# Summed K pairs in Up, one ring of split weight tiles and three rows of 512 in a SwiGLU encoder block

## The chip, the cores and the metric

The kernel runs on one core of a Trainium2 chip. The metric is device time in microseconds (us) of one execution; the number given is the median of several runs. Engines: PE is TensorE (matmuls and transposes), DVE the vector engine, ACT the scalar engine, POOL GpSimd, SP the engine whose queue issues the weight transfers here.

## What is computed

One encoder block on 256 tokens of width 2048, in f32: a hybrid attention layer, a cross-attention layer, and then the part that the change touches, the SwiGLU layer with a hidden width of 5632, and a last norm:

```python
def rms_norm(x, g, eps=NORM_EPS):
    xf = x.astype(jnp.float32)
    y = xf * lax.rsqrt(jnp.mean(xf * xf, axis=-1, keepdims=True) + eps)
    return (y * g.astype(jnp.float32)).astype(x.dtype)
...
x = x + (jax.nn.silu(h @ w_gate) * (h @ w_up)) @ w_down     # h = rms_norm(x, g_f)
```

## The kernel before

Every product of two f32 matrices is made of three matmuls on rounded parts (`mm`, L93 to L95): each operand is split into a high part, a cast made by ACT (L101), and a low part, the difference made by DVE (L102); high by high, high by low and low by high are summed in PSUM. Weights come in pieces of 1 MB into three raw buffers `wraw`, by SP's queue in program order. Each piece of 128x2048 is split in two steps of 1024 columns into tiles `wh` and `wl`, which rotate over four buffers each.

SwiGLU cuts the 5632 hidden columns into one narrow chunk of 512 and five wide chunks of 1024. The chunks run in three groups: the narrow and the first wide one, the second and third, the fourth and fifth. A wide chunk is Gate, then Up (`wide_chunk`, L830); a group ends with its share of the down product (`wide_add`, twice).

`narrow_chunk` (L815) runs the narrow Gate project into two PSUM banks (`acc_4196` and `acc_4197` below), then `normalized_pairs` (L784), which scales x by the rows' norm and makes the operand forms that the wide chunks use, then the narrow Up project (`acc_4401`, `acc_4402`). For each half of the tokens it then applies Silu to Gate's bank (`sg`, ACT, L824), multiplies by Up's (`h`, DVE, L826) and transposes (PE, L325).

A wide Gate or Up (`wide_result`, L742, by `wide_project`, L691) works through 8 pairs of K blocks. A string gives the kind of each pair. A plain pair, "P", has two blocks by two of weights: two splits of 128x1024 and 24 matmuls of 512 columns. A summed pair, "W", uses sums of the blocks (a Winograd form with seven products in place of eight): 21 matmuls; three additions on DVE (L719, 1024 columns; L723 and L724, 512 each) make `tsum` from the raw tile, and four pieces are split: `b11` (raw, 1024), `t13` (sums, 1024), `b21` (raw, 512), `t24` (sums, 1024). Four extra PSUM banks Q take the products shared by several results, from the first W pair to the last; then ACT and DVE read them (`leave`), and after the last pair DVE adds the four plain banks (`join`). The split of `t24` goes to a special pair of tiles, `wh2` and `wl2`, of pool `wsum`, since the four rotating ones are taken.

```python
G_KINDS, U_KINDS = "PPWPWPWP", "PPWPWPPP"
...
t24 = split_blocks(t[:, 2:4, :], wsum)
...
return sb.tile([P, 512], F32, name=name, tag="nat", bufs=7)
```

The last line is `nat` (L168): rows of 128x512 for small results, seven of them in rotation. In SwiGLU its users are `rb` and `rrow` (the norm's factors), `sums` (L682 to L685, one for each summed pair of the operand: three in `normalized_pairs`), `sg` and `h`, and in the wide chunks `sums`, `a21`, `v` and `u`. A new row is written only when the readers of the row that had its buffer are done.

The order of instructions on each engine is set by a scheduler when the program is built, from the order of the code and from the buffers; an engine runs its own list in order, and waits by semaphores where another engine must be done.

## Time and profile before

| | before |
|---|---|
| median of 3 runs | 1153.56 us (1152.98 to 1153.72) |
| the profiled execution's own time | 1152.77 us |
| its span in the profile | 1150.9 us |
| mean granted clock | 0.998 |
| PE, matmuls | busy 1141.8 us, 99%, 5495 instructions |
| DVE | busy 910.8 us, 79% |
| ACT | busy 620.5 us, 54% |
| POOL | busy 68.6 us, 6% |
| moved by DMA | 222.13 MB, mean 193 GB/s |

All durations in the trace are of the one profiled execution. Busy time is the time in which an engine has an instruction in work; the duration printed for a matmul is longer than the step to the next, because matmuls overlap in the engine. A row of a timeline gives start and duration; in brackets stands how long the engine had been idle before it, and what ended that.

### The profile page before, as it was taken

To read this page: it belongs to the slowest core of one execution; us is meant where nothing else is said; L and a number is where in the kernel's file an instruction comes from. 1 tells how busy PE (TensorE), PEld (TensorE's weight loads), DVE (VectorE), ACT (ScalarE), POOL (GpSimd) and SP (SyncE) were. 2 spreads that over 40 slices of the span, in tenths; PEclk is the share of its full clock that TensorE was granted. 3 is DMA by queue.
4 is the path that set the end of the run, shared out by engine and by line. 5 is a ranking of instruction groups with operands and counts; after the bars stand their busy time and mean duration, and the time that the engine had idled before them with its cause. 6 is when DMAs were issued, how large, how long until landed. Compare 5 with 4: busy or idle time off the path is not lost.

```text
span 1150.9 us, 14384 instructions
## 1 busy us (share of the span) xinstructions
PE 1141.8 (99%) x5495; PEld 958.6 (83%) x5495; DVE 910.8 (79%) x1206; ACT 620.5 (54%) x875; POOL 68.6 (6%) x81
## 2 busy tenths in 40 slices
PE   9999999999999999999999999999999999999997
PEld 7888888888888888888888888888888888888887
DVE  6688766586868776988888897997888888988873
ACT  7755454554665555665444564664644554654552
POOL 4920000001000000000000000000000000000021
PEclk9999999999999999999999999999999999999999
DMA  9665334445764445455556555555555555565651
GB/s 355 224 209 188 121 137 165 175 147 194 281 220 165 164 147 183 173 195 209 197 183 214 183 204 198 183 197 205 189 214 191 211 188 190 206 226 204 213 201 73
DMA packets 33764, 222.13 MB, mean 193 GB/s; under 512 B 4128, under 2 KB 4896, under 8 KB 8992
## 3 DMA queue, kind: packets, MB, share of 16 engines
q1 hardware_dynamic: 32256, 216.86, 53.3%
q0 software_dynamic: 864, 3.15, 0.8%
q10 hardware_dynamic: 576, 1.21, 0.3%
q8 instruction: 43, 0.70, 0.2%
q14 instruction: 25, 0.20, 0.0%
HBM read 219.11 MB, written 2.10 MB: 192 GB/s over the span
## 4 chain that ended last, share of the span: by engine, by line
PE 98%; issue 0%; DMA 0%; DVE 0%; ACT 0%; POOLq 0%; POOL 0%; DVEq 0%; ACTq 0%
PE acc L93 27%; PE acc L94 27%; PE acc L95 27%; PE q L93 3%; PE q L94 3%; PE q L95 3%; PE pt L325 2%; PE ppt L472 1%; PE psc L95 1%; PE psc L94 1%; PE psc L93 1%; PE acckv L93 0%; PE acckv L94 0%; PE acckv L95 0%; PE pt L848 0%
## 5 line engine op out<-in xcount | busy, mean ns | idle before, releaser
L101 ACT CAST wh<-wraw 128x1024 fp32r<-128x1024 f32 (+2 forms) x399 | 397.4, 1007 | 388.8 <-PE acc L95 343.3
L102 DVE TENSOR_TENSOR wl<-wraw,wh 128x1024 fp32r<-128x1024 f32 (+2 forms) x399 | 466.8, 1180 | 161.3 <-ACT wh L101 159.7
L94 PE MATMUL acc<-wl,x2n_h 128*128 128x512 f32 x320 | 124.8, 391 | 0.0
L95 PE MATMUL acc<-wh,x2n_l 128*128 128x512 f32 x320 | 124.3, 389 | 0.0
L94 PE MATMUL acc<-wl,hT_h 128*128 128x512 f32 (+1 forms) x272 | 103.7, 382 | 0.0
L95 PE MATMUL acc<-wh,hT_l 128*128 128x512 f32 (+1 forms) x272 | 103.2, 380 | 0.0
L93 PE MATMUL acc<-wh,x2n_h 128*128 128x512 f32 x320 | 102.0, 390 | 0.0
L93 PE MATMUL acc<-wh,hT_h 128*128 128x512 f32 (+1 forms) x272 | 88.5, 380 | 0.0
L94 PE MATMUL acc<-wl,x0T_h 128*128 128x512 f32 x224 | 88.0, 394 | 0.0
L93 PE MATMUL acc<-wh,x0T_h 128*128 128x512 f32 x224 | 87.5, 396 | 0.4 <-ACT x0T_h L104 0.4
L95 PE MATMUL acc<-wh,x0T_l 128*128 128x512 f32 x224 | 87.8, 393 | 0.0
L102 DVE TENSOR_TENSOR wl<-tsum,wh 128x1024 fp32r<-128x1024 f32 x66 | 78.8, 1221 | 8.7 <-ACT wh L101 8.7
L101 ACT CAST wh<-tsum 128x1024 fp32r<-128x1024 f32 x66 | 67.2, 1047 | 17.8 <-PE acc L95 8.1
L93 PEld LDWEIGHTS acc<-wh,x2n_h 128*128 128x128 f32 x320 | 60.1, 188 | 12.5
L95 PEld LDWEIGHTS acc<-wh,x2n_l 128*128 128x128 f32 x320 | 60.1, 188 | 12.3
L94 PEld LDWEIGHTS acc<-wl,x2n_h 128*128 128x128 f32 x320 | 60.1, 188 | 12.2
L93 PEld LDWEIGHTS acc<-wh,hT_h 128*128 128x128 f32 x272 | 51.2, 188 | 9.7
L94 PEld LDWEIGHTS acc<-wl,hT_h 128*128 128x128 f32 x272 | 51.2, 188 | 9.5
L95 PEld LDWEIGHTS acc<-wh,hT_l 128*128 128x128 f32 x272 | 51.2, 188 | 9.4
L94 PE MATMUL acc<-wl,forms_h 128*128 128x512 f32 (+1 forms) x155 | 59.0, 384 | 0.0
L95 PE MATMUL acc<-wh,forms_l 128*128 128x512 f32 (+1 forms) x155 | 58.7, 384 | 0.0
L93 PE MATMUL acc<-wh,forms_h 128*128 128x512 f32 (+1 forms) x155 | 56.1, 384 | 0.0
(369 smaller groups left out, 2218.9 us busy)
## 6 DMA issues: line engine op xcount, KB each, us to landing
wraw<-in_w_gate SPq DMA_DIRECT2D x44, 1024.0 KB, 4.8
wraw<-in_w_up SPq DMA_DIRECT2D x44, 1024.0 KB, 4.8
wraw<-in_w_dn SPq DMA_DIRECT2D x36, 1024.0 KB, 4.9
wraw<-in_w_in SPq DMA_DIRECT2D x24, 1024.0 KB, 4.8
wraw<-in_w_out SPq DMA_DIRECT2D x16, 1024.0 KB, 4.8
wraw<-in_w_down SPq DMA_DIRECT2D x8, 1024.0 KB, 4.8
wraw<-in_w_in_lat SPq DMA_DIRECT2D x7, 832.0 KB, 8.3
wraw<-in_w_xk SPq DMA_DIRECT2D x4, 1024.0 KB, 6.3
```

What stands on the lines that cost most here:

```text
L93: nc.tensor.matmul(o, l.h, r.h, start=start, stop=False)
L94: nc.tensor.matmul(o, l.h, r.l, start=False, stop=False)
L95: nc.tensor.matmul(o, l.l, r.h, start=False, stop=stop)
L101: last_cast[0] = nc.scalar.copy(out=dst.h, in_=src).ins
L102: last_split[0] = nc.vector.tensor_tensor(out=dst.l, in0=src, in1=dst.h.bitcast(F32), op=ALU.subtract).ins
L325: nc.tensor.transpose(out=pt[:, j * P:(j + 1) * P], in_=src[:, j * P:(j + 1) * P], identity=ident)
L472: nc.tensor.transpose(out=pt[:, kt * S + tt * P:kt * S + (tt + 1) * P], in_=p[:, tt, kt * P:(kt + 1) * P], identity=ident)
```

## The change

Up gets the same kinds as Gate: three summed pairs instead of two. Gate takes its pairs in their natural order, Up as 0 2 1 4 3 6 5 7, which by kinds is P W P W P W P P, so that two plain ones come last. The high and the low tiles of split weights come from one ring each, in strict rotation: four tiles up to the end of the attention layers, and six in SwiGLU, where two more are taken from a new pool `late`; the special tiles go, and `t24` takes tiles of the ring as the others do. The rows of `nat` come from pool `early`, seven, until the attention layers are closed, and then from `late`, three. Up's weights are laid out on the host by the new kinds.

```diff
--- before.py
+++ after.py
@@ -36,7 +36,9 @@
 NFC = FF // 512
 NPC = (FF - 512) // 1024
 
-G_KINDS, U_KINDS = "PPWPWPWP", "PPWPWPPP"
+GU_KINDS = "PPWPWPWP"
+G_ORDER, U_ORDER = (0, 1, 2, 3, 4, 5, 6, 7), (0, 2, 1, 4, 3, 6, 5, 7)
 
 DN_KINDS = "PP" + "PPPW" * NPC
 
@@ -87,6 +89,32 @@
     tables = ExitStack()
     tp = tables.enter_context(tc.tile_pool(name="tp", bufs=1))
 
+    class Ring:
+        def __init__(self, name):
+            self.name, self.slots, self.made = name, [], 0
+        def more(self, pool, n):
+            self.slots = [(pool, f"{self.name}{self.made + i}") for i in range(n)] + self.slots
+            self.made += n
+        def next(self):
+            self.slots.append(self.slots.pop(0))
+            pool, tag = self.slots[-1]
+            return pool.tile([P, 1024], F32R, name=self.name, tag=tag, bufs=1)
+    w_high, w_low = Ring("wh"), Ring("wl")
+    w_high.more(wp, 4)
+    w_low.more(wp, 4)
+    nat_pool = [early, 7]
+    def split_tile(n, ncols):
+        return Split(*[ring.next()[:, :n * ncols].rearrange("p (k c) -> p k c", k=n) for ring in (w_high, w_low)])
 
     def mm(o, l, r, start, stop):
 
@@ -133,12 +161,7 @@
         step = max(1, 1024 // ncols // 2 * 2)
         for k in range(0, nk, step):
             n = min(step, nk - k)
-            if pool:
-                w = pool((P, n, ncols), "w")
-            else:
-                w = [wp.tile([P, 1024], F32R, name=x, tag=x, bufs=4)[:, :n * ncols].rearrange("p (k c) -> p k c", k=n)
-                     for x in ("wh", "wl")]
-                w = Split(*w)
+            w = pool((P, n, ncols), "w") if pool else split_tile(n, ncols)
             if fine:
                 for j in range(n):
                     for c in ([slice(0, ncols)] if cut is None or k + j else [slice(0, cut), slice(cut, ncols)]):
@@ -166,7 +189,8 @@
         return accs
 
     def nat(name):
-        return sb.tile([P, 512], F32, name=name, tag="nat", bufs=7)
+        pool, bufs = nat_pool
+        return pool.tile([P, 512], F32, name=name, tag="nat", bufs=bufs)
 
 
     banks = [(pacc, "acc"), (pps, "ps")]
@@ -642,7 +666,10 @@
         lambda oc: project(lambda kt: xoT[:, kt, :], [a["w_xo"][oc, 0]]), g_f, "x2T", x2raw)
     soft_pool.close()
     attention.close()
-    wsum = ctx.enter_context(tc.tile_pool(name="wsum", bufs=1))
+    late = ctx.enter_context(tc.tile_pool(name="late", bufs=1))
+    nat_pool[:] = late, 3
+    w_high.more(late, 2)
+    w_low.more(late, 2)
 
 
     def pair_raw(src):
@@ -651,14 +678,8 @@
         tc.keep_in_program_order(nc.sync.dma_start(out=raw, in_=src))
         return raw
 
-    def w_tile(n=2, pool=None):
-        pool, tags, bufs = (wp, ("wh", "wl"), 4) if pool is None else (pool, ("wh2", "wl2"), 1)
-        return Split(*[pool.tile([P, 1024], F32R, name=x, tag=x, bufs=bufs)[:, :n * 512].rearrange(
-            "p (b c) -> p b c", b=n) for x in tags])
-    def split_blocks(src, pool=None):
-        w = w_tile(src.shape[1], pool)
+    def split_blocks(src):
+        w = split_tile(src.shape[1], 512)
         split_into(w, src)
         return w
 
@@ -714,7 +735,7 @@
                 continue
             if i == summed[0]:
                 Q = {q: ps_tile(f"q{q}") for q in (1, 5, 7, 6)}
-            t = wsum.tile([P, 4, 512], F32, name="tsum", tag="tsum", bufs=1)
+            t = late.tile([P, 4, 512], F32, name="tsum", tag="tsum", bufs=1)
             b11 = split_blocks(raw[:, 1:3, :])
             nc.vector.tensor_tensor(out=t[:, 0:2, :], in0=raw[:, 1:3, :],
                                     in1=raw[:, 0:1, :].to_broadcast([P, 2, 512]), op=ALU.add)
@@ -722,7 +743,7 @@
             b21 = split_blocks(raw[:, 3:4, :])
             nc.vector.tensor_tensor(out=t[:, 2, :], in0=t[:, 0, :], in1=raw[:, 2, :], op=ALU.add)
             nc.vector.tensor_tensor(out=t[:, 3, :], in0=t[:, 2, :], in1=raw[:, 3, :], op=ALU.add)
-            t24 = split_blocks(t[:, 2:4, :], wsum)
+            t24 = split_blocks(t[:, 2:4, :])
             own = i == summed[0], i == summed[-1]
             A11, A12, A21, A22, S5, S6, S7, S3 = [pairs[i].forms[:, n, :] for n in range(8)]
             mm(Q[1], A11, b11[:, 0, :], *own)
@@ -739,7 +760,7 @@
                 join(tt, oc, accs[tt][oc])
         banks.reverse()
 
-    def wide_result(pairs, src, kinds):
+    def wide_result(pairs, src, order, kinds):
 
         res = []
 
@@ -756,7 +777,7 @@
             r = res[tt][:, oc, :]
             nc.vector.tensor_tensor(out=r, in0=acc, in1=r, op=ALU.subtract if (tt, oc) == (1, 0) else ALU.add)
 
-        wide_project(pairs, src, range(len(pairs)), kinds, leave, join)
+        wide_project(pairs, src, order, kinds, leave, join)
         return res
 
     def wide_add(pairs, src, order, kinds, oc0, done=None):
@@ -797,13 +818,13 @@
             nc.vector.tensor_tensor(out=xr, in0=xr, in1=rrow[:, :S].unsqueeze(1).to_broadcast([P, 4, S]), op=ALU.mult)
         pairs = []
         t, n = None, 4
-        for i, kind in enumerate(G_KINDS):
+        for i, kind in enumerate(GU_KINDS):
             xr = x2raw[i // 2][:, i % 2 * 2:i % 2 * 2 + 2, :]
             if kind == "P":
-                if n == 4 and "P" in G_KINDS[i + 1:]:
+                if n == 4 and "P" in GU_KINDS[i + 1:]:
                     t, n = act_tile(name="x2n"), 0
                 elif n == 4:
-                    t = Split(*[wsum.tile([P, 2, S], F32R, name="odd" + x, tag="odd" + x, bufs=1) for x in "hl"])
+                    t = Split(*[late.tile([P, 2, S], F32R, name="odd" + x, tag="odd" + x, bufs=1) for x in "hl"])
                     n = 0
                 split_into(t[:, n:n + 2, :], xr)
                 pairs.append(Pair(t[:, n:n + 2, :]))
@@ -829,11 +850,11 @@
 
     def wide_chunk(c, spare):
 
-        g = wide_result(xn, a["w_gate"][c], G_KINDS)
+        g = wide_result(xn, a["w_gate"][c], G_ORDER, GU_KINDS)
         for tt in range(NT):
             for oc in range(2):
                 nc.scalar.activation(g[tt][:, oc, :], g[tt][:, oc, :], AF.Silu)
-        u = wide_result(xn, a["w_up"][c], U_KINDS)
+        u = wide_result(xn, a["w_up"][c], U_ORDER, GU_KINDS)
         t = act_tile(name="hT")
         pts = []
         for oc in range(2):
@@ -992,8 +1013,8 @@
         "w_xo": _pieces(i["w_xo"][0]),
         "w_gate0": _pieces(i["w_gate"][0][:, :512]),
         "w_up0": _pieces(i["w_up"][0][:, :512]),
-        "w_gate": _pairs(i["w_gate"][0][:, 512:], G_KINDS),
-        "w_up": _pairs(i["w_up"][0][:, 512:], U_KINDS),
+        "w_gate": _pairs(i["w_gate"][0][:, 512:], GU_KINDS),
+        "w_up": _pairs(i["w_up"][0][:, 512:], GU_KINDS),
         "w_dn": _pairs(i["w_down"][0], DN_KINDS),
         "w_down": _pieces(i["w_down"][0][-2048:, 1024:]).transpose(1, 0, 2, 3, 4),
     }
```

ACT, from the end of the narrow Up project to the first wide Gate. `wh_4507` and `wh_4511` are the last tiles of the narrow Up's weights, `wh_4571` to `wh_4609` those of the wide Gate's first two pairs, `wh_4644` and `wh_4649` the first two of its summed pair; `sg_4541` is the first Silu. Before:

```order
L824 ACT_TABLE_LOAD
L824 ACTIVATE sg_4541<-acc_4196,x2Tr_4186 128x512
L101 CAST forms_h_4384<-x2T_f_4161 128x256 x2
L101 CAST wh_4507<-wraw_4505 128x1024
L101 CAST wh_4511<-wraw_4505 128x1024
L101 CAST wh_4571<-wraw_4569 128x1024
L101 CAST wh_4575<-wraw_4569 128x1024
L101 CAST wh_4605<-wraw_4603 128x1024
L101 CAST forms_h_4352<-sums_4354 128x512
L101 CAST forms_h_4369<-sums_4371 128x512
L101 CAST forms_h_4384<-sums_4386 128x512
L824 ACTIVATE sg_4552<-acc_4197,x2Tr_4186 128x512
```

Now:

```order
L129 CAST wh_4571<-wraw_4569 128x1024
L129 CAST wh_4575<-wraw_4569 128x1024
L129 CAST wh_4605<-wraw_4603 128x1024
L129 CAST wh_4609<-wraw_4603 128x1024
L129 CAST wh_4644<-wraw_4637 128x1024
L129 CAST forms_h_4352<-sums_4354 128x512
L129 CAST wh_4649<-tsum_4643 128x1024
L129 CAST forms_h_4369<-sums_4371 128x512
L129 CAST forms_h_4384<-sums_4386 128x512
L845 ACT_TABLE_LOAD
L845 ACTIVATE sg_4541<-acc_4196,x2Tr_4186 128x512
L845 ACTIVATE sg_4552<-acc_4197,x2Tr_4186 128x512
```

The first Silu and its table load stood ahead of all casts of the wide Gate's tiles; now they stand behind five of them, behind the cast of the `tsum` and behind the three casts of `forms` from `sums`.

PE, at the end of the narrow Up project (`acc_4401`, `acc_4402`) and the start of the wide Gate (`acc_4565`, which gets the PSUM bank that `acc_4196`, the narrow Gate's first result, had). Before, the first instruction of the wide Gate stood some way ahead, and here the rest follows:

```order
L93 MATMUL acc_4401<-wh_4507,x2T_h_4159 128x512
L93 MATMUL acc_4402<-wh_4507,x2T_h_4159 128x512
L93 MATMUL acc_4565<-wh_4571,x2n_h_4346 128x512
L94 MATMUL acc_4401<-wl_4508,x2T_h_4159 128x512
L95 MATMUL acc_4401<-wh_4507,x2T_l_4160 128x512
```

and

```order
L93 MATMUL acc_4402<-wh_4511,x2T_h_4159 128x512
L94 MATMUL acc_4402<-wl_4512,x2T_h_4159 128x512
L95 MATMUL acc_4402<-wh_4511,x2T_l_4160 128x512
L94 MATMUL acc_4565<-wl_4572,x2n_h_4346 128x512
L95 MATMUL acc_4565<-wh_4571,x2n_l_4347 128x512
```

Now:

```order
L122 MATMUL acc_4402<-wl_4512,x2T_h_4159 128x512
L123 MATMUL acc_4402<-wh_4511,x2T_l_4160 128x512
L121 MATMUL acc_4565<-wh_4571,x2n_h_4346 128x512
L122 MATMUL acc_4565<-wl_4572,x2n_h_4346 128x512
L123 MATMUL acc_4565<-wh_4571,x2n_l_4347 128x512
L121 MATMUL acc_4565<-wh_4575,x2n_h_4346 128x512
L122 MATMUL acc_4565<-wl_4576,x2n_h_4346 128x512
```

The first matmul on `acc_4565` moved behind the last matmul that reads `wh_4511`.

DVE, in the same place. Before:

```order
L102 TENSOR_TENSOR wl_4606<-wraw_4603,wh_4605 128x1024
L102 TENSOR_TENSOR forms_l_4353<-sums_4354,forms_h_4352 128x512
L826 SCALAR_TENSOR_TENSOR h_4543<-acc_4401,x2Tr_4186,sg_4541 128x512
L102 TENSOR_TENSOR forms_l_4370<-sums_4371,forms_h_4369 128x512
L102 TENSOR_TENSOR forms_l_4385<-sums_4386,forms_h_4384 128x512
L719 TENSOR_TENSOR tsum_4643<-wraw_4637 128x1024
L826 SCALAR_TENSOR_TENSOR h_4554<-acc_4402,x2Tr_4186,sg_4552 128x512
L102 TENSOR_TENSOR wl_4610<-wraw_4603,wh_4609 128x1024
```

Now:

```order
L130 TENSOR_TENSOR wl_4645<-wraw_4637,wh_4644 128x1024
L130 TENSOR_TENSOR forms_l_4353<-sums_4354,forms_h_4352 128x512
L744 TENSOR_TENSOR tsum_4643<-tsum_4643,wraw_4637 128x512
L130 TENSOR_TENSOR wl_4650<-tsum_4643,wh_4649 128x1024
L130 TENSOR_TENSOR forms_l_4370<-sums_4371,forms_h_4369 128x512
L130 TENSOR_TENSOR forms_l_4385<-sums_4386,forms_h_4384 128x512
L745 TENSOR_TENSOR tsum_4643<-tsum_4643,wraw_4637 128x512
L847 SCALAR_TENSOR_TENSOR h_4543<-acc_4401,x2Tr_4186,sg_4541 128x512
L847 SCALAR_TENSOR_TENSOR h_4554<-acc_4402,x2Tr_4186,sg_4552 128x512
```

The product `h_4543`, which reads the first Silu, stood between the splits of `forms`; now it stands behind all of them, and behind the split `wl_4650` of the `tsum`.

## Rows read from the trace of the kernel before

**Rows 1.** The page, part 1: busy time, share of the span and instructions of each engine

```profile
PE 1141.8 (99%) x5495; PEld 958.6 (83%) x5495; DVE 910.8 (79%) x1206; ACT 620.5 (54%) x875; POOL 68.6 (6%) x81
```

**Rows 2.** Waits of PE over the whole span: us in total, times, longest

```profile
PE wps L207 <- DVE warm L201: 1.2, 1, 1.2
PE acc L93 <- ACT x0T_h L104: 0.4, 1, 0.4
PE po L93 <- ACT val_h L104: 0.2, 1, 0.2
```

**Rows 3.** Timeline of PE, 443.9 to 457.2: start, us, engine, line; 56 rows between

```profile
444.01 0.39 PE L95 MATMUL acc<-wh,x2T_l 128*128 128x512 f32 x1
...
456.93 0.39 PE L95 MATMUL acc<-wh,x2T_l 128*128 128x512 f32 x1
```

**Rows 4.** DVE by line and form: count | busy us, mean ns | idle before, releaser

```profile
L102 DVE TENSOR_TENSOR wl<-wraw,wh 128x1024 fp32r<-128x1024 f32 x349 | 427.3, 1233 | 140.2 <-ACT wh L101 138.7
L102 DVE TENSOR_TENSOR wl<-tsum,wh 128x1024 fp32r<-128x1024 f32 x66 | 78.8, 1221 | 8.7 <-ACT wh L101 8.7
L719 DVE TENSOR_TENSOR tsum<-wraw 128x1024 f32<-128x1024 f32 x33 | 40.4, 1224 | 6.0 <-DMA wraw<-in_w_up 3.8 <-DMA wraw<-in_w_gate 1.2 <-DMA wraw<-in_w_dn 0.7
L102 DVE TENSOR_TENSOR wl<-wraw,wh 128x512 fp32r<-128x512 f32 x34 | 23.5, 690 | 14.8 <-ACT wh L101 14.8
L723 DVE TENSOR_TENSOR tsum<-tsum,wraw 128x512 f32<-128x512 f32 x33 | 22.7, 688 | 0.4
```

**Rows 5.** Windows: us, busy of PE, PEld, DVE, ACT, POOL; PEclk, DMA share, GB/s

```profile
718.00:762.00 44.00, 44.00 (x203) 36.54 (x202) 40.49 (x52) 25.82 (x33) 0.00 (x0) 1.00 0.55 192
762.00:804.00 42.00, 42.00 (x187) 34.78 (x186) 34.42 (x39) 21.06 (x23) 0.00 (x0) 1.00 0.57 200
480.00:1140.00 660.00, 660.00 (x3034) 550.44 (x3033) 551.56 (x640) 343.37 (x404) 12.96 (x8) 1.00 0.56 195
```

**Rows 6.** Timeline of ACT, 462 to 500

```profile
466.85 1.28 ACT L824 ACT_TABLE_LOAD   x1
468.15 0.69 ACT L824 ACTIVATE sg<-acc,x2Tr 128x512 f32<-128x512 f32 x1
...
477.59 1.05 ACT L101 CAST wh<-wraw 128x1024 fp32r<-128x1024 f32 x1 [1.92 <-PE acc L95]
478.55 1.65 ACT L101 CAST forms_h<-sums 128x512 fp32r<-128x512 f32 x3
480.11 0.68 ACT L824 ACTIVATE sg<-acc,x2Tr 128x512 f32<-128x512 f32 x1
...
485.06 0.59 ACT L101 CAST hT_h<-pt 128x512 fp32r<-128x512 f32 x1 [3.34 <-PE pt L325]
```

**Rows 7.** Timeline of PE, 478.5 to 486

```profile
479.88 0.39 PE L95 MATMUL acc<-wh,x2T_l 128*128 128x512 f32 x1
480.11 0.39 PE L94 MATMUL acc<-wl,x2n_h 128*128 128x512 f32 x1
...
484.43 0.60 PE L325 MATMUL pt<-ident,h 128*128 128x128 f32 x4
```

**Rows 8.** Timeline of PE, first matmuls and the last one

```profile
1.18 3.59 PE L207 MATMUL wps<-warm 128*128 128x512 bf16 x8 [1.18 <-DVE warm L201]
5.16 1.22 PE L93 MATMUL acc<-wh,x0T_h 128*128 128x512 f32 x2 [0.39 <-ACT x0T_h L104]
...
1143.34 0.28 PE L95 MATMUL acc<-w_h,forms_l 128*128 128x256 f32 x1
```

**Rows 9.** Windows after the last matmul, columns as in rows 5

```profile
1144.00:1146.00 2.00, 0.00 (x0) 0.00 (x0) 1.30 (x5) 0.73 (x1) 0.55 (x1) 1.00 0.48 186
1146.00:1148.00 2.00, 0.00 (x0) 0.00 (x0) 0.55 (x2) 0.21 (x1) 0.00 (x0) 0.69 0.75 281
```

**Rows 10.** Timeline of DVE, 700 to 770

```profile
709.09 1.23 DVE L102 TENSOR_TENSOR wl<-wraw,wh 128x1024 fp32r<-128x1024 f32 x1 [3.54 <-ACT wh L101]
...
765.85 1.22 DVE L102 TENSOR_TENSOR wl<-tsum,wh 128x1024 fp32r<-128x1024 f32 x1 [1.12 <-ACT wh L101]
```

## The prediction

> **What bounds the kernel now.** I read the page's first part, then TensorE's waits, its timeline, the vector and scalar engines by form, windows over the last two thirds of the program, and finally the timelines around 480 us, where the order of work changes most. PE is busy for 1141.8 us [rows 1] of a span of 1150.9. Its whole list of waits has three entries, 1.2, 0.4 and 0.2 us, all of them in stages far from the edited ones or in the start [rows 2]. From 480 to 1140 us it is busy for 660.00 of 660 us at granted clock 1.00, the 2.4 GHz level, while DVE works 551.56 us and ACT 343.37 us [rows 5]. So the kernel is bound by TensorE's own pace: a matmul taken away is worth its full time, and any new wait of TensorE is lost in full, since nothing later can make it good. The reader should therefore look for two things only: matmuls removed, and new places where PE must stop.
>
> **The pace.** Matmuls of 512 columns start 57 steps apart from 444.01 to 456.93 us [rows 3], which is 12.92 / 57 = 0.2267 us each. The 0.39 printed for one is its pipelined duration, not its pace.
>
> **What is removed from PE.** A plain K pair issues 24 such matmuls and a summed one 21 (eight products of three against seven of three). Each of the five wide chunks turns one more pair of Up from plain to summed, so 15 matmuls go: 15 x 0.2267 = **-3.40 us**.
>
> **What is added on DVE and ACT.** A plain pair splits two raw tiles of 1024 columns. A summed one splits one raw tile of 1024, one of 512 and two summed tiles of 1024, and makes three additions. By the means of DVE [rows 4] (both 512 additions at the 0.688 of L723) the difference is 1.233 + 2 x 1.221 + 0.690 + 1.224 + 2 x 0.688 - 2 x 1.233 = 4.50 us a pair, 22.5 us in all. DVE then stands at 574 of 660 us, 87 per cent. In the Up stage of the third chunk, 762 to 804 us, it would be 34.42 + 4.50 = 38.9 us in a stretch that becomes 0.7 us shorter, 41.3 us; the stretch that holds the end of Gate and the start of Up, 718 to 762, is already at 40.49 of 44 [rows 5]. ACT makes at most ten more casts of about 1.05 us [rows 6], 10.5 us on 343 of 660. I cost all of this at nothing. The cover is TensorE's own work in the same stretch, and if it failed, PE would wait for a low tile `wl`; that is a rival below. SP and POOL issue the same transfers and operations as before, and each transfer is of the same size.
>
> The ring of six in place of four and a special one lets casts run further ahead, so raw buffers come free and transfers start earlier. PE waits for no transfer and no cast in this stage now [rows 2], so this too is worth nothing. The other moves (two splits of Up's weights ahead of additions in the stage before SwiGLU) shift DVE work by an operation or so under matmuls and are costed at nothing.
>
> **What the three rows of 512 add: a new wait.** The rows rotate, so a new one is written only when the reader of the one three places back is done. In the narrow chunk the sequence is `rb`, `rrow`, three `sums`, then `sg`, `h`, `sg`, `h`. The first `sg` now takes the row of the first `sums`, whose last reader is the split into `forms`; with seven rows it had a free one. On ACT the first Silu therefore moves from its place ahead of the casts of Gate's tiles to a place behind five of them, behind three casts of `forms`, and behind the cast `wh_4649<-tsum_4643`. That cast takes the ring's slot of `wh_4511`, six back, and the last reader of `wh_4511` is the last matmul of the narrow chunk's Up project. So the first Silu cannot run before that project has ended. But TensorE's next matmul, `acc_4565`, writes the bank of `acc_4196`, the narrow Gate's result, which that Silu reads. Before, this Silu ran at 468.15 us [rows 6], twelve microseconds early. Now PE has to stand still.
>
> How long: the last Up matmul starts at 479.88 and lasts 0.39 [rows 7], so the result is in at 480.27. A hand-over between PE and ACT takes 0.03 us: transposes end at 484.43 + 0.60 = 485.03 [rows 7] and the cast that reads them starts at 485.06 [rows 6]. Then ACT runs the cast (477.59 to 478.55, 0.96), two casts of `forms` (three from 478.55 to 480.11, so 0.52 each), the table load (466.85 to 468.15, 1.30) and the Silu (0.69) [rows 6], and hands over: 480.27 + 0.03 + 0.96 + 1.04 + 1.30 + 0.69 + 0.03 = 484.32. The matmul that started at 480.11 [rows 7] would start there: **+4.21 us**. Behind it all of TensorE's remaining program is queued. Bounds: if the table load ran during the wait, 1.30 less, 2.9 us; if the cast also had to wait for an addition of DVE, 1.22 more [rows 4], 5.4 us. I take 4.21, for each link is an instruction that stands in the order and has its own row. While PE stands, DVE and ACT catch up, so nothing is late next.
>
> **The sum.** The profiled execution took 1152.77 us: 1152.77 - 3.40 + 4.21 = 1153.58. The median of the three runs, 1153.56, is 0.79 above that execution, so on its footing 1154.4, with 2.9 and 5.4 us of stall 1153.1 and 1155.6. What a measurement of this kernel can tell from no change is about 0.2 per cent: 1151.25 to 1155.87. By this sum the gain and the wait cancel.
>
> **Rivals.** *The clock falls in the new pause (slower).* After the last matmul, started at 1143.34 [rows 8], the granted clock was 1.00 in the window 1144 to 1146 and averaged 0.69 in 1146 to 1148 [rows 9], so it went to the lower level, 1.2 GHz, after PE had been idle between 2.4 and 4.4 us. A pause of 4.2 us lies inside these bounds, near the upper one. If it falls, the first matmuls behind the pause run at half pace. The start of the program shows the price: eight warm matmuls in 3.59 us and the next two in 1.02 (5.16 to 6.18, that is 1.22 less about 0.2 of overlap) [rows 8], in place of 10 x 0.2267 = 2.27, so some 2.35 us more; about half of it, 1.2 us, if the clock recovers soon. That gives 1155.6 to 1156.8. Against it: there is one fall to go by, and the pause may be shorter than 4.2. The Trainium skill, page "TensorE: Matmul & The Clock Gate", section "Why this matters for your kernels", warns that a pause between bursts of matmuls puts the engine back to the slow clock; by that rule this rival would be the forecast, at 1155.6 to 1156.8. No row here shows a pause in the middle of the kernel, so I leave it as a rival.
>
> *DVE too late in Up.* In a second chunk of a group (the third and the fifth) Up's first summed pair comes one plain pair earlier, 24 x 0.2267 = 5.44 us, while DVE has only one pair's two splits less to do before it, 2 x 1.233. That takes 2.97 us from its lead, and ahead of the split at 765.85 it had 1.12 us idle [rows 10]: up to 1.85 us late. If PE feels it in both chunks, up to 3.7 us, half of that as a middle: 1154.4 + 1.85 = 1156.3, at most 1158.1. Against it: DVE stood idle for 3.54 us at 709.09, waiting for a cast [rows 10], and six slots let these casts come earlier. It decides when the lead lost exceeds the lead that the ring gives.
>
> *No pause.* If a bank is free earlier than I read, or the Silu is not held up, only the matmuls count: 1153.56 - 3.40 = 1150.2, faster. For it speaks that PE showed no wait here; against it, that the places of the Silu on ACT and of the slot's reader on PE are fixed by the order.
>
> **How the numbers follow.** The forecast (pause, clock stays) gets 0.48, the falling clock 0.30, DVE's lateness 0.12, no pause 0.10. Predicted is the forecast's 1154.4. Faster is the last rival, 0.10. Same takes nearly all of the forecast, 0.46, and 0.06 from the low ends of the two slow rivals, 0.52. Slower is what is left, 0.38. The range runs from 1152.5 (the forecast's 1153.1, less 0.6 for the spread of the runs, 1152.98 below 1153.56) to 1157.1 (the falling clock's 1156.8 and a little of its spread). It leaves out the fast rival and the top of DVE's, under 2 in 10.
>
> **What would show it.** In the profile after: PE with 15 matmuls fewer and a wait of its `acc` matmul for ACT's `sg` of about 4.2 us close to 480 us; ACT's table load and first Silu behind the cast of a `tsum`, after the last narrow Up matmul; DVE some 22 us busier. A granted clock below 1.00 in windows just behind the pause shows the first rival; waits of PE for `wl` or `wh` in Up of the third and fifth chunk show the second. No wait of PE for `sg`, and a time near 1150, would prove the main step wrong.

## The result

The changed kernel takes **1158.49 us** (median of 6 runs, 1157.51 to 1159.59) against 1153.37 for the kernel before (6 runs): a ratio of 1.0045, 95% interval 1.0033 to 1.0057. It is slower by about 5.1 us, outside the range that was given. The profiled execution is the fastest of the six, 1157.51 us, with a span of 1155.7; its mean granted clock is 0.998, that of the other five 0.995.

The first part of the page of the changed kernel, busy time of the engines, answers to [rows 1]: 15 instructions fewer on PE, 18.9 us more on DVE.

```profile
PE 1141.3 (99%) x5480; PEld 956.8 (83%) x5480; DVE 929.7 (80%) x1231; ACT 625.6 (54%) x885; POOL 67.7 (6%) x81
```

The waits of PE over the whole span (us in total, times, longest) answer to [rows 2]. Two are new: one of 4.2 us for the first Silu, and two, 1.1 us together, for a cast.

```profile
PE acc L121 <- ACT sg L845: 4.2, 1, 4.2
...
PE q L121 <- ACT wh L129: 1.1, 2, 0.7
...
```

The timeline of PE around the first (columns as in [rows 7]) shows the pause and, behind it, matmuls at another pace: up to 487.68 they start 0.42 to 0.43 us apart, from 488.03 on 0.23 again.

```profile
479.68 0.39 PE L123 MATMUL acc<-wh,x2T_l 128*128 128x512 f32 x1
484.28 0.62 PE L121 MATMUL acc<-wh,x2n_h 128*128 128x512 f32 x1 [4.22 <-ACT sg L845]
484.70 0.63 PE L122 MATMUL acc<-wl,x2n_h 128*128 128x512 f32 x1
...
487.68 0.51 PE L123 MATMUL acc<-wh,x2n_l 128*128 128x512 f32 x1
488.03 0.40 PE L121 MATMUL acc<-wh,x2n_h 128*128 128x512 f32 x1
```

The windows there (columns as in [rows 5]) show why. The granted clock is full while PE stands idle, goes down as the work comes back, to 0.63 and 0.52 on average, at the lower level of 1.2 GHz nearly all of 486 to 488, and is full again after 488.

```profile
482.00:484.00 2.00, 0.00 (x0) 0.00 (x0) 2.00 (x4) 1.97 (x3) 0.00 (x0) 1.00 0.47 197
484.00:486.00 2.00, 1.72 (x5) 1.32 (x6) 2.00 (x4) 0.92 (x2) 0.00 (x0) 0.63 0.00 0
486.00:488.00 2.00, 2.00 (x6) 1.60 (x5) 1.01 (x2) 0.00 (x0) 0.00 (x0) 0.52 0.00 0
488.00:490.00 2.00, 2.00 (x10) 1.65 (x9) 0.00 (x0) 0.00 (x0) 0.00 (x0) 1.00 0.00 0
```

ACT in that place, to be read against [rows 6]: the cast of the `tsum` that waits for the end of the narrow Up, two casts of `forms`, the table load, the Silu. That is the chain of the prediction, link by link. The bracket of the first row names an addition of DVE; in the program this cast waits for two other engines, DVE's addition that makes its `tsum`, which ended at 479.91, and TensorE's last matmul that reads `wh_4511`, which ended later, at 480.07. The margin was narrow: with that addition 0.2 us later DVE would have set the start.

```profile
480.14 1.04 ACT L129 CAST wh<-tsum 128x1024 fp32r<-128x1024 f32 x1 [1.19 <-DVE sums L706]
481.10 1.13 ACT L129 CAST forms_h<-sums 128x512 fp32r<-128x512 f32 x2
482.25 1.28 ACT L845 ACT_TABLE_LOAD   x1
483.54 0.69 ACT L845 ACTIVATE sg<-acc,x2Tr 128x512 f32<-128x512 f32 x1
```

The other new waits, in the timeline of PE, stand in Up of the third and of the fifth chunk:

```profile
773.51 0.39 PE L123 MATMUL q<-wh,forms_l 128*128 128x512 f32 x1
774.29 0.73 PE L121 MATMUL q<-wh,forms_h 128*128 128x512 f32 x2 [0.40 <-ACT wh L129]
...
1028.54 0.39 PE L123 MATMUL q<-wh,forms_l 128*128 128x512 f32 x1
1029.60 0.73 PE L121 MATMUL q<-wh,forms_h 128*128 128x512 f32 x2 [0.67 <-ACT wh L129]
```

**Where 4.8 us come from.** From the starts of the stages in PE's timeline:

| | before | after | difference |
|---|---|---|---|
| first matmul of the wide Gate | 480.11 | 484.28 | +4.17 |
| first down product | 564.51 | 569.86 | +5.35 |
| second group's Gate | 630.28 | 635.64 | +5.36 |
| second down product | 799.42 | 804.12 | +4.70 |
| third group's Gate | 885.59 | 890.31 | +4.72 |
| third down product | 1054.69 | 1059.43 | +4.74 |
| last matmul | 1143.34 | 1148.13 | +4.79 |

The 15 matmuls are worth -3.40. The pause costs the step 479.68 to 484.28 less an ordinary one, 4.60 - 0.23 = +4.37. Nine steps from 484.28 to 488.03 take 3.75 in place of 2.04: +1.71 for the clock. The second group has six matmuls fewer (-1.36) but is only 0.66 shorter: +0.70. The third group is not shorter at all (169.12 after, 169.10 before): +1.38. Together -3.40 + 4.37 + 1.71 + 0.70 + 1.38 = +4.76, of 4.79 seen. This is the account of the profiled execution. The other five, at a mean clock of 0.995, probably lost more than 1.71 to the clock: the profiled execution of the run `natord` below, also at 0.995, lost 2.49 (twelve steps from 484.17 us take 5.21 in place of 2.72).

### The profile page after: what moved, and what is told of

The parts are those of the page before. It is cut to its first block, busy times and chain, and to the rows that moved or that the text cites. A ratio compares the mean times of both kernels' runs of the same rounds, so it can differ in the third digit from the quotient of the medians.

```text
span 1155.7 us, 14395 instructions
## 1 busy us (share of the span) xinstructions
PE 1141.3 (99%) x5480; PEld 956.8 (83%) x5480; DVE 929.7 (80%) x1231; ACT 625.6 (54%) x885; POOL 67.7 (6%) x81
## 4 chain that ended last, share of the span: by engine, by line
PE 94%; DVE 3%; ACT 1%; DMA 1%; issue 1%; POOLq 0%; POOL 0%; DVEq 0%; ACTq 0%
PE acc L122 26%; PE acc L123 26%; PE acc L121 26%; PE q L121 3%; PE q L122 3%; PE q L123 3%; PE pt L349 2%; DVE wl L130 1%; ACT wh L129 1%; PE ppt L496 1%; DMA wraw<-in_w_up 1%; PE psc L123 1%; PE psc L122 1%; PE psc L121 1%; PE acckv L121 0%
## 5 line engine op out<-in xcount | busy, mean ns | idle before, releaser
L129 ACT CAST wh<-wraw 128x1024 fp32r<-128x1024 f32 (+2 forms) x399 | 391.0, 1002 | 371.7 <-PE acc L123 306.0
L121 PE MATMUL acc<-wh,x2n_h 128*128 128x512 f32 x320 | 113.0, 393 | 4.2 <-ACT sg L845 4.2
L130 DVE TENSOR_TENSOR wl<-tsum,wh 128x1024 fp32r<-128x1024 f32 x76 | 91.9, 1220 | 9.4 <-ACT wh L129 9.3
L121 PE MATMUL acc<-wh,hT_h 128*128 128x512 f32 (+1 forms) x272 | 95.8, 380 | 0.0
L129 ACT CAST wh<-tsum 128x1024 fp32r<-128x1024 f32 x76 | 79.5, 1052 | 29.4 <-PE acc L123 10.6
L121 PE MATMUL acc<-wh,x0T_h 128*128 128x512 f32 x224 | 87.4, 396 | 0.4 <-ACT x0T_h L132 0.4
L121 PEld LDWEIGHTS acc<-wh,x2n_h 128*128 128x128 f32 x320 | 60.5, 189 | 17.3 <-ACT sg L845 4.6
L122 PE MATMUL q<-wl,forms_h 128*128 128x512 f32 x152 | 59.2, 389 | 0.0
L121 PEld LDWEIGHTS acc<-wh,hT_h 128*128 128x128 f32 x272 | 51.2, 188 | 9.6
L123 PE MATMUL q<-wh,forms_l 128*128 128x512 f32 x152 | 58.7, 389 | 0.0
L740 DVE TENSOR_TENSOR tsum<-wraw 128x1024 f32<-128x1024 f32 x38 | 46.4, 1222 | 11.8 <-DMA wraw<-in_w_up 7.0
```

Of the source, the lines that this page charges most:

```text
L121: nc.tensor.matmul(o, l.h, r.h, start=start, stop=False)
L122: nc.tensor.matmul(o, l.h, r.l, start=False, stop=False)
L123: nc.tensor.matmul(o, l.l, r.h, start=False, stop=stop)
L129: last_cast[0] = nc.scalar.copy(out=dst.h, in_=src).ins
L130: last_split[0] = nc.vector.tensor_tensor(out=dst.l, in0=src, in1=dst.h.bitcast(F32), op=ALU.subtract).ins
L740: nc.vector.tensor_tensor(out=t[:, 0:2, :], in0=raw[:, 1:3, :], in1=raw[:, 0:1, :].to_broadcast([P, 2, 512]), op=ALU.add)
```

## Experiments

The kernel before, timed beside each of them, has a median of 1153.4 to 1153.5 us. "Change" is the changed kernel, 1158.5.

### The three parts of the loss

**One more row**

```diff
-    nat_pool[:] = late, 3
+    nat_pool[:] = late, 4
```

> Theory: the loss of the changed kernel has three parts that add up: 4.2 to 4.4 us of pause near 480 us (first Silu held by the row of the first sums), 1.7 to 2.7 us of matmuls at the lower clock behind it, about 2.1 us of late casts of tsum in Up of the third and fifth chunk. With a fourth row the first Silu moves ahead of the casts, the second stays behind them, so the pause shrinks to 0 to 1.3 us and the granted clock stays 1.00 from 480 to 492; the time falls from 1158.5 by 3.1 to 4.4 and by 1.7 to 2.7, to 1151.4 to 1153.7. Rival: the pause alone is what the row costs and the rest is work on DVE all over Up: 1154.1 to 1155.4.

Measured: 1152.49 us, ratio to before 0.9992 (0.9983 to 1.0001): 6.0 us less than the change, by one row of 512. In PE's waits the Silu costs 0.6 us in place of 4.2, and the windows from 480 to 492 us are all at clock 1.00. The waits for casts in Up stay:

```profile
PE q L121 <- ACT wh L129: 0.7, 1, 0.7
PE acc L121 <- ACT sg L845: 0.6, 1, 0.6
PE acc L121 <- ACT wh L129: 0.5, 2, 0.3
```

So the row makes the pause, and the pause takes the clock with it. The last part is another matter.

**Keep TensorE busy in the pause**

```diff
         ua = project(x2T, [a["w_up0"][0, i] for i in range(4)])
+        fill = ps_tile("fill")
+        for i in range(18):
+            nc.tensor.matmul(fill, xn[0].plain.h[:, 0, :P], xn[0].plain.h, start=True, stop=True)
```

> 18 extra matmuls of 512 columns (18 x 0.2267 = 4.1 us) into an unused bank stand between the narrow Up project and the wide Gate; nothing reads them. The wait for the Silu stays, the engine is only kept busy meanwhile. Theory: the wide Gate starts at the same 484.3 us, the granted clock stays at 1.00, the first matmuls run 0.227 apart, and the time falls by 1.7 to 2.7 us to 1155.8 to 1156.8. Rival: the slow steps behind the pause have another cause than the pause of TensorE (the engines that feed it): the steps stay 0.427 apart and the time stays at 1158.5.

Measured: 1155.09 us, 3.4 less than the change with 18 matmuls more; that saves somewhat more than the 1.7 to 2.7 expected. PE's timeline: the first real matmul comes 4.62 us after the last one of Up, as in the change (4.60), but the next follow at 0.23 to 0.34.

```profile
480.58 0.39 PE L123 MATMUL acc<-wh,x2T_l 128*128 128x512 f32 x1
480.81 4.24 PE L843 MATMUL fill<-x2n_h 128*128 128x512 f32 x18
485.20 0.50 PE L121 MATMUL acc<-wh,x2n_h 128*128 128x512 f32 x1
485.54 0.39 PE L122 MATMUL acc<-wl,x2n_h 128*128 128x512 f32 x1
```

Its windows there are at full clock; the first of them:

```profile
484.00:486.00 2.00, 1.85 (x8) 1.22 (x7) 2.00 (x4) 1.20 (x3) 0.00 (x0) 1.00 0.00 0
```

The slow steps are the clock's, and here the clock followed TensorE's idleness. The profiled execution of this run also lost less in the second and third group (0.87 us by the count above, 2.08 in the change). So of the 3.4 us the clock's 1.7 is shown in two traces, and it was probably more in the median of the change; why less was lost in the groups, no run tells.

**The rows alone, in the kernel before**

```diff
+    nat_pool[:] = wsum, 3
...
-        return sb.tile([P, 512], F32, name=name, tag="nat", bufs=7)
+        pool, bufs = nat_pool
+        return pool.tile([P, 512], F32, name=name, tag="nat", bufs=bufs)
```

> The kernel before with three rows in SwiGLU in place of seven and nothing else. Theory: the first Silu is held behind the cast wh_4609, four back of which is wh_4511; after the end of the narrow Up come that cast, the table load and the Silu: 0.03 + 0.96 + 1.30 + 0.69 + 0.03 = 3.0, so TensorE pauses for 3.0 to 3.3 us; with the clock up 1156.4 to 1156.7, with the clock down for 1.7 to 2.7 behind it 1158.1 to 1159.4. Rival: the rows alone hold nothing, it takes the ring too: 1153.4.

Measured: 1156.60 us, +3.2. Its five executions took 1156.37, 1156.58, 1156.60, 1158.05 and 1158.46; the profiled one is that of 1158.05. It shows the pause, 3.19 us, and then, unlike the change, some matmuls at full pace before the clock goes down:

```profile
479.80 0.39 PE L96 MATMUL acc<-wh,x2T_l 128*128 128x512 f32 x1
483.38 0.50 PE L94 MATMUL acc<-wh,x2n_h 128*128 128x512 f32 x1 [3.19 <-ACT sg L827]
...
484.64 0.43 PE L96 MATMUL acc<-wh,x2n_l 128*128 128x512 f32 x1
484.87 0.63 PE L94 MATMUL acc<-wh,x2n_h 128*128 128x512 f32 x1
```

```profile
482.00:484.00 2.00, 0.62 (x3) 0.54 (x4) 2.00 (x3) 1.89 (x3) 0.00 (x0) 1.00 0.55 234
484.00:486.00 2.00, 2.00 (x8) 1.64 (x7) 2.00 (x4) 0.00 (x0) 0.00 (x0) 0.71 0.27 41
```

The pause is as worked out, 3.0 to 3.3. Two of five executions are 1.5 to 2 us longer than the others; that the clock stayed up in those others fits but was not profiled, and their mean granted clock, 0.998 as in the profiled one, does not tell.

**The third summed pair alone, in the buffers before**

```diff
-G_KINDS, U_KINDS = "PPWPWPWP", "PPWPWPPP"
+G_KINDS, U_KINDS = "PPWPWPWP", "PPWPWPWP"
+U_ORDER = (0, 2, 1, 4, 3, 6, 5, 7)
```

> The kernel before with Up's third summed pair and its new order alone: four rotating tiles and the special one, seven rows. Theory: no pause near 480 us and no lower clock; the 15 matmuls are worth 3.4 us, and what the late casts in Up give back is 0.9 to 2.8 (as the runs with 18 filling matmuls and with four rows showed): 1150.9 to 1152.8. Rival: without the ring of six the third pair is too late everywhere: above 1153.4. Rival: the late casts come from the ring itself, none here: 1150.0.

Measured: **1150.31 us**, ratio 0.9972 (0.9960 to 0.9983): -3.1 of the possible -3.4. That is below the range of the theory; the last rival was right. The second and third group take 167.77 and 167.74 us, 1.37 and 1.36 less than before: the matmuls' full worth. PE's list of waits is that of the kernel before, nothing in Up:

```profile
PE wps L208 <- DVE warm L202: 1.2, 1, 1.2
PE acc L94 <- ACT x0T_h L105: 0.6, 1, 0.6
PE po L94 <- ACT val_h L105: 0.2, 1, 0.2
```

So in the old buffers the splits and additions that the change adds cost nothing, and the waits in Up come with the new buffers.

**Old kinds of Up, new ring, three rows**

```diff
-        u = wide_result(xn, a["w_up"][c], U_ORDER, GU_KINDS)
+        u = wide_result(xn, a["w_up"][c], U_ORDER, "PPWPWPPP")
...
-G_ORDER, U_ORDER = (0, 1, 2, 3, 4, 5, 6, 7), (0, 2, 1, 4, 3, 6, 5, 7)
+G_ORDER, U_ORDER = (0, 1, 2, 3, 4, 5, 6, 7), (0, 1, 2, 3, 4, 5, 6, 7)
```

> Up with its two summed pairs in the natural order as before; ring of six and three rows as in the changed kernel. Theory: 15 matmuls come back (+3.4 us), the late casts go (-2.1): only pause and lower clock stand against the kernel before, 1153.4 + 4.4 + 1.7 to 2.7 = 1159.5 to 1160.5. Rival, the third summed pair saves nothing at all: 1158.5; rival, the ring of six or the rows cost something in the other chunks too: above 1161.

Measured: 1159.13 us, 0.4 below the range of the theory. The second and third group take 169.13 and 169.10 us, as before: with two summed pairs in Up the ring costs nothing, and pause and clock alone are +5.75.

### Why TensorE waits for casts in Up

The chain of the changed kernel that ended last, in order of time, from the end of Gate in the fifth chunk (start, us, what). ACT's cast of a `tsum` waits for TensorE to leave a slot of the ring; behind its split stand three more on DVE, an addition, a reading of Q and one more split, which ends at 1015.02 and frees a raw buffer; only then the next load of Up is issued, and it lands 6.73 us later. The chain goes on over DVE to the cast that TensorE waits for at 1029.60:

```profile
1006.12 0.24 PE q L123
...
1006.43 1.06 ACT wh L129
...
1007.52 0.99 DVE wl L130
...
1008.66 3.32 DVE wl L130 x3
...
1012.06 1.22 DVE tsum L740
1013.28 0.60 DVE res L771
1013.88 1.14 DVE wl L130
...
1015.04 6.73 DMA wraw<-in_w_up
...
1021.87 0.63 ACT wh L129
...
1028.51 1.05 ACT wh L129
```

That chain tells what the cast waited for, not that it came later than in the old buffers. By the tiles' numbers in the program, TensorE waits in both chunks for the first of the two `tsum` tiles (`t13`) of Up's second summed pair. Its cast in the third chunk, in the change and in the kernel with the third pair alone:

```profile
773.19 1.05 ACT L129 CAST wh<-tsum 128x1024 fp32r<-128x1024 f32 x1 [0.28 <-issue]
768.65 1.04 ACT L102 CAST wh<-tsum 128x1024 fp32r<-128x1024 f32 x1
```

The first product that reads it starts at 774.29 in the change, as shown above, and in the kernel with the third pair alone here:

```profile
773.39 0.39 PE L94 MATMUL q<-wh,forms_h 128*128 128x512 f32 x1
```

Windows of PE from the group's first matmul to that product, in the same order (us, busy and matmuls, clock, DMA share, GB/s):

```profile
635.64:774.28 138.64, 138.26 (x618) 1.00 0.52 190
631.00:773.38 142.38, 142.38 (x637) 1.00 0.56 197
```

Counted from the group's first matmul (635.64 and 631.00), the cast ends at 138.60 us in the change and at 138.69 in the old buffers: it is not late. But the product stands 19 places further ahead in TensorE's list, 4.3 us of work. In the fifth chunk it is 19 places again, and the cast ends 0.57 us later (139.24 against 138.67). What moved is the order of work, on all three engines: at that place in the old buffers TensorE is busy with the plain pair before, and that pair's first low tile comes later in the change, 138.32 us from the start of the group against 136.59.

**Order of the pairs.** In the change (the run `natord`):

```diff
-G_ORDER, U_ORDER = (0, 1, 2, 3, 4, 5, 6, 7), (0, 2, 1, 4, 3, 6, 5, 7)
+G_ORDER, U_ORDER = (0, 1, 2, 3, 4, 5, 6, 7), (0, 1, 2, 3, 4, 5, 6, 7)
```

> Up in the natural order of its pairs (P P W P W P W P), all else as in the changed kernel. Theory: the summed pair of Up stands third again, one plain pair later, so the waits of 0.40 and 0.67 us for the cast of tsum near 774 and 1029 us are gone, and with them about 2.1 us: 1156.0 to 1157.5; pause and lower clock near 484 us unchanged. Rival: DVE has too much to do in Up with three summed pairs wherever they stand: waits of TensorE elsewhere in Up, time 1158.5 or above.

Measured: 1163.39 us, 4.9 above the change; in its profiled execution the second and third group take 169.68 and 170.57 us. The same order in the old buffers, `U_ORDER` natural in the kernel with the third pair alone:

> The kernel before with Up's third summed pair in the natural order P P W P W P W P. Theory: with one plain pair at the end the reading of the Q banks collides with the next stage as in the run of the ring in natural order (5 us above the change): above 1150.3 by 2 to 5 us, 1152.3 to 1155.3. Rival: that collision came from the ring too: 1150.3 as with the new order.

Measured: 1150.78 us. And two summed pairs side by side, `U_ORDER` (0, 1, 2, 4, 3, 6, 5, 7), in the kernel with four rows:

> Four rows, Up's pairs as P P W W P W P P: the first summed pair one plain pair later than in the change, the last one in the same place. Theory: the backlog of DVE where Gate ends and Up begins is what makes the first summed pair late; with 5.4 us more the waits near 769 and 1024 go: 1150.3 to 1151.5 against 1152.5. Rival: two summed pairs in a row are 2 x 9.7 us of DVE work on 9.5 us of matmuls and TensorE waits there: above 1152.5.

Measured: 1154.88 us, 2.4 above four rows alone. In the ring both other orders are worse; in the old buffers the order hardly matters (0.5 us). The theory that the earlier first summed pair is what is late falls.

**Less work on DVE**, in the kernel with four rows:

```diff
-            nc.vector.tensor_tensor(out=t[:, 2, :], in0=t[:, 0, :], in1=raw[:, 2, :], op=ALU.add)
-            nc.vector.tensor_tensor(out=t[:, 3, :], in0=t[:, 2, :], in1=raw[:, 3, :], op=ALU.add)
+            nc.gpsimd.tensor_tensor(out=t[:, 2, :], in0=t[:, 0, :], in1=raw[:, 2, :], op=ALU.add)
+            nc.gpsimd.tensor_tensor(out=t[:, 3, :], in0=t[:, 2, :], in1=raw[:, 3, :], op=ALU.add)
```

> Four rows, and the two additions of 512 columns of each summed pair on POOL in place of DVE (1.38 us less DVE work a pair; POOL takes about 2.0 us for such an addition elsewhere in this kernel, DVE 0.69). Theory: DVE's backlog at the end of Gate and the start of Up is what makes the casts late, so the waits near 769 and 1024 us shrink: 1150.3 to 1151.5 against 1152.5 with four rows. Rival: the sums come later by 2 x 1.3 us, and TensorE waits for the last tile of each summed pair: 1152.5 or more, up to 1160.

Measured: 1164.32 us; PE waits 7.5 us for low tiles `wl`. The rival came true, beyond its 1160, so this run says nothing of DVE's load.

**A ring of five, seven rows**

```diff
-    nat_pool[:] = late, 3
-    w_high.more(late, 2)
-    w_low.more(late, 2)
+    nat_pool[:] = late, 7
+    w_high.more(late, 1)
+    w_low.more(late, 1)
```

> Seven rows and a ring of five tiles, else the changed kernel: neither Silu is held. Theory: no wait for a Silu at all (0.65 us left with four rows): 1151.8 if a ring of five serves Up as well as one of six. Rival: the sixth tile is what gives the casts their lead, and the waits in Up grow: above 1152.5.

Measured: 1156.35 us. No wait for a Silu, but PE's timeline has steps of about 0.37 us or more in each of the five wide chunks: five single tiles serve them worse than six.

**The special pair again** beside a ring of five, with four rows and with three; `own` takes tiles `wh2` and `wl2` of `late`:

```diff
-    w_high.more(late, 2)
-    w_low.more(late, 2)
+    w_high.more(late, 1)
+    w_low.more(late, 1)
...
-            t24 = split_blocks(t[:, 2:4, :])
+            t24 = split_blocks(t[:, 2:4, :], own=True)
```

> The changed kernel with four rows and, in the same memory, a ring of five and the special pair of tiles for t24 again. Theory: in the strict ring the cast of t24 has to wait until TensorE is done with the tile six back, and stands between the Silus of Gate; with a tile of its own it runs ahead, the waits in Up are gone, and neither Silu is held: 1153.4 - 3.4 = 1150.0 to 1150.8. Rival: it is the seven rows of the kernel before that saved the run with Up alone, or five tiles are too few: 1152 or above (five without the special pair gave 1156.4).

> As the run before, with three rows: only the pause is left in. Theory: the first Silu is held behind the cast wh_4644, five back of which is wh_4511, so the pause is the same 4.2 us, the clock falls behind it for 1.7 to 2.7, and Up has no waits: 1150.4 + 4.4 + 1.7 to 2.7 = 1156.5 to 1157.5. Rival: pause and ring share one cause, the waits in Up come from the late start: 1158.5.

Measured: 1153.15 and 1159.88 us. Both miss: the waits in Up are still there (with four rows 2.1 us for the casts that Q products read, in a profiled execution of 1155.56 us, the slowest of eleven). That `t24` has no tile of its own is not the cause. The pause with three rows is 4.2 us, as expected.

**Same tiles, same rows, two ways to hand them out.** `sp4n4` is the edit just shown with four rows and without the two `more` lines: four tiles of the class `Ring`, where each slot is a buffer of its own, and the special pair. `up4` is the kernel with the third pair alone and `nat_pool[:] = wsum, 4`: the four tiles are one rotating set.

```diff
-            pool, tag = self.slots[-1]
-            return pool.tile([P, 1024], F32R, name=self.name, tag=tag, bufs=1)
+                w = [wp.tile([P, 1024], F32R, name=x, tag=x, bufs=4)[:, :n * ncols].rearrange("p (k c) -> p k c", k=n)
+                     for x in ("wh", "wl")]
```

> The changed kernel with the buffers of the kernel before except the rows: ring of four and the special pair for t24, four rows. Theory: it is the tiles beyond four, with the order of casts and splits that they bring, that make the loads of Up late (the second tile of a summed pair waits for its slot, the splits behind it on DVE free the raw buffer late); without them Up has no waits: 1150.0 to 1151.0. Rival: the fewer rows or the way in which the ring takes its tiles do it: 1152.5 to 1153.5 as with five and the special pair.

> The run with Up's third summed pair alone, with four rows in place of seven. Theory: four rows are enough in the wide chunks and for the first Silu: 1150.3, at most 0.7 more where the second Silu is held. Rival: the rows are what the waits in Up come from: 1152.5 or above.

Measured: 1153.18 us and **1149.88 us** (ratio 0.9969, 0.9958 to 0.9980, the fastest of all). Neither number of tiles nor rows: only the class is left, 3.3 us. ACT at the start of Up in the third chunk, and the product that reads the tile cast last, in `sp4n4`:

```profile
762.77 1.06 ACT L129 CAST wh<-wraw 128x1024 fp32r<-128x1024 f32 x1 [0.30 <-PE acc L123]
765.68 1.74 ACT L129 CAST wh<-wraw 128x512 fp32r<-128x512 f32 x2 [1.85 <-PE acc L123]
...
768.37 1.03 ACT L129 CAST wh<-wraw 128x1024 fp32r<-128x1024 f32 x1
769.45 0.50 PE L121 MATMUL q<-wh,forms_h 128*128 128x512 f32 x1 [0.33 <-ACT wh L129]
```

and the same place in `up4`:

```profile
761.33 0.62 ACT L103 CAST wh<-wraw 128x512 fp32r<-128x512 f32 x1 [0.22 <-PE acc L97]
764.45 2.01 ACT L103 CAST wh<-wraw 128x1024 fp32r<-128x1024 f32 x2 [2.50 <-PE acc L97]
...
767.41 1.04 ACT L103 CAST wh<-wraw 128x1024 fp32r<-128x1024 f32 x1
770.82 0.39 PE L95 MATMUL q<-wh,forms_h 128*128 128x512 f32 x1
```

In `up4` the 512 columns of `b21` are cast at 761.33, ahead of the two tiles of the plain pair behind it. In `sp4n4` the second tile of that plain pair goes first, at 762.77, and `b21` waits for a slot until 765.68. Counted from the first matmul of the group (630.70 in `up4`, 632.13 in `sp4n4`) that is 2.92 us later. But no product waits for `b21` here. TensorE waits for the tile cast in the last row, and that cast is not late: counted from the group's first matmul it ends at 137.27 us in `sp4n4` and at 137.75 in `up4`. Its first product, though, stands 15 places further ahead in TensorE's list in `sp4n4`, and TensorE waits 0.33 us for it. The other two waits are of the same kind (PE q L121 <- ACT wh L129: 1.4 us in three waits): in the first chunk 0.73 us, with the product 12 places further ahead, in the fifth 0.33, with 15. Counted as steps longer than 0.2267, the three waits and the step behind each are 2.2 us, of 2.9 between the two profiled executions. So the single buffers of the ring let the scheduler build other orders, and at these three places it is TensorE's own order that asks too early. Why the scheduler puts the products there, no run shows.

**All casts in order**, in `sp4n4` and in the kernel with four rows, for the split tiles of SwiGLU:

```diff
-            last_cast[0] = nc.scalar.copy(out=dst.h, in_=src).ins
+            cast = nc.scalar.copy(out=dst.h, in_=src)
+            last_cast[0] = cast.ins
+            if keep:
+                tc.keep_in_program_order(cast)
```

> As sp4n4 (ring of four single tiles, special pair, four rows), with the casts of the split weight tiles of SwiGLU kept in the order of the program on ACT. Theory: up4 and sp4n4 have the same number of tiles and rows and differ by 3.3 us; in sp4n4 each tile is a buffer of its own, so the scheduler puts casts of later tiles ahead of earlier ones (the second tile of a plain pair ahead of a piece of the summed pair before it), and TensorE waits for those left behind. In order, the waits near 535, 769 and 1023 us go: 1150 to 1151.5. Rival: the order of the casts is not it, another engine's order is (DVE's splits and sums): 1153.2; or casts kept in order stand behind Silus and copies and TensorE waits more: above 1153.5.

> As rows4 (ring of six, four rows), with the casts kept in the order of the program. Theory: the waits near 769, 1018 and 1024 us go; both narrow Silus now stand ahead of the wide Gate's casts, and these behind the forms of the sums, which may cost a new wait of 1 to 3 us near 480: 1150.5 to 1153. Rival: waits in Up as before, 1152.5 and more.

Measured: 1240.54 and 1230.66 us. Kept in order, the casts of the next stage come too late, and PE waits for `wh` for 44.9 and 38.9 us; in the first of the two the casts for the first wide Up come behind four Silus of Gate, and PE waits 4.39 us, to 531.50. That is the second rival of the first of the two. These runs do not say what the order of the casts is worth by itself.

## Why the prediction was wrong

- **Pace and matmuls removed: right.** 15 fewer, -3.40; alone they gave -3.1 and, with four rows, -3.6.
- **DVE and ACT at nothing: right.** The extra work (forecast 22.5 us, the whole of DVE rose by 18.9) makes no wait in the old buffers.
- **The new wait: right.** Place, chain and size: restart at 484.28 forecast 484.32, wait 4.22 forecast 4.21. That the bound of 5.4, with an addition of DVE in the chain, did not come in was a matter of 0.16 us. With one row more the wait shrinks to 0.6.
- **The ring "worth nothing", the step that failed.** "PE waits for no transfer and no cast in this stage now, so this too is worth nothing" looked only for a gain. A new ring also changes the order in which the scheduler puts the casts, the splits and TensorE's own products, and through the three raw buffers the loads. With three summed pairs in Up that cost 2.1 us in the profiled execution (0.70 + 1.38).
- **The rival of DVE's lateness** had the stage (Up of the third and fifth chunk) and, by luck, the price (2.08, 1.85 forecast), but not the cause. The longest waits are at the second summed pair, not the first, and neither DVE's added work nor the earlier first pair is enough to make them, as the third pair alone and in both orders shows.
- **The falling clock, left out of the sum that gave 1154.4,** was given 0.30 and 1.2 to 2.35 us; it fell, for 1.71 in the profiled execution. As said there, by the rule of the Trainium skill (page "TensorE: Matmul & The Clock Gate", section "Why this matters for your kernels": keep pauses between bursts of matmuls short, or the engine goes back to the slow clock) this case was the forecast. The trace agrees with the page, with 0.63 and 0.52 of granted clock behind a pause of 4.22 us; it should have been the likeliest case.
- **How the numbers followed, the second step that failed.** Pause, clock and lateness were weighed as alternatives, each added to the forecast by itself. They do not exclude each other: the pause came, the clock fell behind it, and time was lost in Up for a cause of its own. 1154.4 + 1.71 + 2.08 = 1158.2, the 1158.49 measured within 0.3; with the 1.71 probably larger in the median, that close a fit is in part luck. The top of the range, 1157.1, held one of them at a time.

## What to carry to other kernels

Where one engine is busy for 99 per cent, follow each buffer that gets smaller to the instruction that must wait for it: here one row of 512 columns decided 6 us. Rivals that hang on different causes add up; give the sum a chance of its own, and let the range reach it. Change the kinds of work and the buffers in separate steps: the third summed pair alone, in the old tiles with four rows, is 3.6 us faster than the kernel before; with the new ring and four rows 0.9 of that was left, too little to tell from nothing (0.9983 to 1.0001).

## What the runs showed of the hardware

In the profiled execution of the kernel with three rows alone, TensorE's clock stayed up for some matmuls behind the pause of 3.19 us and fell only then: steps were 0.23 up to 484.87 and about 0.43 from there on. Behind 4.22 us the lower level did not last equally long: the profiled execution of the change lost 1.71 us by it; in that of `natord` the clock fell while TensorE still stood idle (to 484.17), the granted clock was 0.61 in 482 to 484, 0.50 from 484 to 488 and 0.68 in 488 to 490, and 2.49 us were lost. Behind the 0.65 us of the kernel with four rows it stayed at 1.00.
